# Memory's output projection of twelve token tiles by seven products per pair of tiles, its weights partly loaded again for each pair

## The chip, the cores and the metric

The kernel runs on one core of one Trainium2 chip. The metric is the time of one execution on the device in microseconds, the median of several runs. The program is one launch; all stages follow each other on the same five engines: TensorE (PE), VectorE (DVE), ScalarE (ACT), GpSimd (POOL) and SyncE (SP, which here only issues DMAs).

## The reference, cut to what matters

One layer of an encoder: a mixing block, cross attention to 256 memory tokens, and a SwiGLU feed-forward network, each with a residual. There are 2048 tokens of width 1024, four memory heads of width 128, and a feed-forward width of 2816. The change is in the last line of the middle part, the product with `w_mem_out` (512 x 1024).

```python
h = h + jnp.einsum('bsc,cd->bsd', jnp.concatenate([fox, pool], axis=-1), w_out[l])

hn = rmsnorm(h, g_mem_q[l])
...
pm = jax.nn.softmax(sc, axis=-1).astype(mv.dtype)
mo = jnp.einsum('bhsm,bmhd->bshd', pm, mv).reshape(B, S, MEM_WIDTH)
h = h + jnp.einsum('bsc,cd->bsd', mo, w_mem_out[l])

hn = rmsnorm(h, g_ffn[l])
gu = jnp.einsum('bsd,df->bsf', hn, w_gate_up[l])
```

## The kernel before, in words

**The product.** Every large product is done in words of `fp32r`: an operand is split into a rounded high word (a cast on ACT) and the rest as a low word (`sub_hi`, a subtraction on DVE), and `mm3` (lines 57 to 62) multiplies high by high (L60), high by low (L61) and low by high (L62). So one step of a product is three matmuls of 128 x 128 by up to 512 columns.

**The stages.** First come the projections and the forgetting attention (FoX) with the pooling. Then comes the memory stage, in which the change lies. Then the feed-forward network (FFN), whose products are themselves done by Strassen's seven products over halves of tokens and features; its first products are the `bk` matmuls.

**The memory stage** is one loop over the 16 token tiles of 128 tokens (n = 0 to 16 before). It is a software pipeline that is written out by hand: PE and SP run in program order (`with in_order(EN.SP)`), and the order on DVE, ACT and POOL is left to a scheduler. In iteration n stand, for different tiles: `query_norm(n)` (24 matmuls, the query projection), `ffn_turn(n-5)` (8 transposes of the finished tile, whose results go to DRAM as `hTd` for the FFN), `load_tile(n+1)` and `out_fox(n+1)` (the residual `h1` is loaded from DRAM into one of six buffers, and the output projection of FoX is added to it), `mem_values` for a pair of tiles (its result, `mo`, is split on the way out of PSUM), `softmax(n-1)`, `weights_tm(n-2)` (8 transposes of the softmax's weights `pm`), `mem_out(n-4, 0)` and `mem_out(n-4, 1)` (the projection that the change is about), `query(n+1)` (sum of squares on ACT, 8 transposes) and `query_t(n)` (4 transposes).

`mem_out(i, a)` gives the 512 columns a of tile i: four heads by `mm3`, 12 matmuls into a bank of the tag `mm` (two of them), and one DVE add of the bank to `h1`. With a = 1 the tile is finished: it is stored (`h2d`) and normed for the FFN (`hn`). The eight pieces of `w_mem_out` lie split in SBUF (`wm`).

**The tail.** In the last iterations the token operands of the FFN are prepared beside the memory stage: `token_ops` loads four raw pieces of 128 x 512 for each of four groups j from `hTd` (`xraw`, two buffers of 1 MB), and splits them and their sums and differences on ACT and DVE into the slabs `qs`, `kh`, `kl`, `cb`; two of the results (s3, s4) go to DRAM by POOL. Which call of `tokens(1)` stands where in the loop sets when SP reaches these loads. `weights_raw` loads the first FFN weight (`graw`, 1 MB) and `weight_ops` prepares it. After the last `mem_out` the FFN's `bk` matmuls begin.

## Time and profile before

| what | us |
|---|---|
| median of 3 runs (2565.06 to 2567.35) | 2566.49 |
| the profiled execution | 2566.67 |
| its span in the profile | 2565.0 |
| PE busy in the span | 2532.6 |
| DVE busy | 1702.0 |
| ACT busy | 1248.6 |
| POOL busy | 802.2 |

The granted TensorE clock was 0.999 of full speed over the span. "Busy" counts an instruction from its start to its modelled end; matmuls overlap, so the distance from start to start is what one of them takes. "Idle before" in brackets is the time that an engine waited ahead of an instruction, with what ended the wait. The DMA share is the mean busy share of the core's 16 DMA engines.

### The profile page before, as it was taken

The page shows a single profiled execution, that of the slowest core. Times are in us where ns is not written, and L with a number is a line of the kernel's source. Part 1 is how long each engine was busy: PE and PEld are TensorE (multiplying, and loading weights), DVE is VectorE, ACT ScalarE, POOL GpSimd, SP SyncE. Part 2 cuts the span into 40 slices and gives each one's busy share as a digit, 9 for nine tenths or more (in the row PEclk, how much of TensorE's full clock was granted, in tenths as well). Part 3 has the DMA queues.
Part 4 walks back from the last instruction along what each step waited for, and adds up shares of the span by engine and source line. Part 5 has one row for each costly group of instructions (what it writes and reads, how often), then busy time and mean ns, then how long its engine had stood idle before and what let it go on. Part 6 is the DMA issues. An engine that isn't in the chain of part 4 may idle for free.

```text
span 2565.0 us, 36894 instructions
## 1 busy us (share of the span) xinstructions
PE 2532.6 (99%) x13133; PEld 2176.9 (85%) x13133; DVE 1702.0 (66%) x2943; ACT 1248.6 (49%) x2375; POOL 802.2 (31%) x1075
## 2 busy tenths in 40 slices
PE   8999999999999999999999999999999999999999
PEld 7999999978888878888778888888888888888887
DVE  6444376569999975555777777756766666665554
ACT  6454452158888865444543433334543333333443
POOL 3334240035455433333334545430001222222000
PEclk9999999999999999999999999999999999999999
DMA  6443375346445242222465455447773332334766
GB/s 244 128 122 117 110 227 175 128 135 166 124 113 160 61 133 80 86 78 87 177 223 183 170 180 189 152 162 268 248 263 119 112 115 103 120 106 169 237 207 205
DMA packets 204777, 396.20 MB, mean 154 GB/s; under 512 B 24368, under 2 KB 99888, under 8 KB 193840
## 3 DMA queue, kind: packets, MB, share of 16 engines
q1 hardware_dynamic: 175088, 296.30, 35.9%
q0 software_dynamic: 29504, 97.54, 9.9%
q8 instruction: 103, 1.69, 0.3%
q14 instruction: 82, 0.67, 0.1%
HBM read 268.85 MB, written 124.91 MB: 154 GB/s over the span
## 4 chain that ended last, share of the span: by engine, by line
PE 84%; issue 9%; DVE 3%; DMA 2%; ACT 1%; POOL 1%; SPq 0%; POOLq 0%; DVEq 0%; ACTq 0%
PE bk L60 13%; PE bk L62 13%; PE bk L61 13%; PE acc L752 5%; PE sps L689 5%; PE tp L767 4%; PE zps L60 4%; PE zps L61 4%; PE zps L62 4%; PE mmps L62 3%; PE mmps L60 3%; PE mmps L61 3%; PE oo L62 1%; PE oo L60 1%; PE oo L61 1%
## 5 line engine op out<-in xcount | busy, mean ns | idle before, releaser
L55 DVE TENSOR_TENSOR ww<-draw,ww 128x512 fp32r<-128x512 f32 x308 | 204.7, 703 | 156.1 <-ACT ww L178 155.7
L178 ACT CAST ww<-draw 128x512 fp32r<-128x512 f32 x308 | 179.4, 620 | 219.6 <-PE bk L62 176.4
L55 DVE TENSOR_TENSOR ww<-graw,ww 128x512 fp32r<-128x512 f32 x220 | 175.9, 806 | 105.9 <-ACT ww L178 105.5
L61 PE MATMUL bk<-ww,ww 128*128 128x512 f32 x616 | 239.6, 389 | 0.0
L60 PE MATMUL bk<-ww,ww 128*128 128x512 f32 x616 | 239.6, 389 | 0.0
L62 PE MATMUL bk<-ww,ww 128*128 128x512 f32 x616 | 239.6, 389 | 0.0
L178 ACT CAST ww<-graw 128x512 fp32r<-128x512 f32 x220 | 135.9, 622 | 180.4 <-PE bk L62 159.4
L55 DVE TENSOR_TENSOR pl<-tp,ph 128x512 fp32r<-128x512 f32 (+3 forms) x298 | 177.8, 599 | 24.1 <-ACT ph L783 22.4
L702 ACT ACTIVATE s<-s,mx 128x1024 f32<-128x1024 f32 (+2 forms) x192 | 173.8, 906 | 4.2 <-DVE mx L696 2.3
L60 PE MATMUL zps<-wh,xhi 128*128 128x386 f32 x512 | 175.7, 343 | 0.1
L61 PE MATMUL zps<-wl,xhi 128*128 128x386 f32 x512 | 173.6, 339 | 0.0
L62 PE MATMUL zps<-wh,xl 128*128 128x386 f32 x512 | 173.2, 338 | 0.0
L767 PE MATMUL tp<-ident,s 128*128 128x128 f32 x1088 | 171.5, 273 | 1.7 <-DVE pl L55 1.1
L783 ACT CAST ph<-tp 128x512 fp32r<-128x512 f32 (+3 forms) x298 | 149.8, 515 | 33.4 <-PE tp L767 28.6
L767 PEld LDWEIGHTS tp<-ident,s 128*128 128x128 f32 x1088 | 133.0, 140 | 31.2 <-DVE pl L55 6.4
L62 PE MATMUL bk<-qs,ww 128*128 128x512 f32 x352 | 137.2, 390 | 1.1 <-DVE ww L55 1.1
L60 PE MATMUL bk<-qs,ww 128*128 128x512 f32 x352 | 137.9, 392 | 0.3 <-ACT s L1318 0.3
L1399 POOL DMA_DIRECT2D out_dram<-o x32 | 17.3, 542 | 382.6 <-DVE o L1396 376.8
L61 PE MATMUL bk<-kh,ww 128*128 128x512 f32 x352 | 137.0, 389 | 0.0
L60 PE MATMUL bk<-kl,ww 128*128 128x512 f32 x352 | 136.9, 389 | 0.0
L61 PE MATMUL bk<-cb,ww 128*128 128x512 f32 x352 | 136.9, 389 | 0.0
L62 PE MATMUL bk<-kl,ww 128*128 128x512 f32 x352 | 136.9, 389 | 0.0
(548 smaller groups left out, 7234.7 us busy)
## 6 DMA issues: line engine op xcount, KB each, us to landing
graw<-in_w_gu_dram SPq DMA_DIRECT2D x44, 1024.0 KB, 5.5
draw<-in_w_down_dram SPq DMA_DIRECT2D x66, 256.0 KB, 4.1
xl<-in_xT_dram SPq DMA_DIRECT2D x64, 256.0 KB, 4.6
qkT<-st SPq DMA_DIRECT2D x64, 256.0 KB, 2.7
wdr<-in_w_down_dram SPq DMA_DIRECT2D x22, 512.0 KB, 4.3
vd<-cb SPq DMA_DIRECT2D x16, 512.0 KB, 3.2
xr<-in_x_dram SPq DMA_DIRECT2D x16, 512.0 KB, 3.3
qs<-qkT SPq DMA_DIRECT2D x8, 1024.0 KB, 6.8
```

The costliest lines, as they stand in the source:

```text
L55: (eng or dve).tensor_tensor(out=lo, in0=src, in1=f(hi), op=ALU.subtract)
L60: pe.matmul(ps, lhsT=sh, rhs=mh, start=first, stop=False, skip_group_check=goes_on)
L61: pe.matmul(ps, lhsT=sh, rhs=ml, start=False, stop=False, skip_group_check=goes_on)
L62: pe.matmul(ps, lhsT=sl, rhs=mh, start=False, stop=last, skip_group_check=goes_on)
L178: act.copy(hi, raw)
L689: pe.matmul(ps[:, :wn], lhsT=qs[:, i * P:(i + 1) * P], rhs=kk[:, 512 * c:512 * c + wn], start=(a == 0), stop=(a == 1))
L702: act.activation(s[:, sl], s[:, sl], AF.Exp, bias=ng, scale=-1.0, accum_out=l[:, q, g:g + 1])
L752: pe.matmul(acc[:, qa * P:], lhsT=v[:, j, :], rhs=pm[:, qa * P:], start=state["n"] == 1, stop=state["n"] == 2 * nk)
L767: pe.transpose(tp[:, q * P:(q + 1) * P], unit["rows"][q][:, j * P:(j + 1) * P], ident[:])
L783: act.copy(ph[:, sl], tp[:, sl])
L1399: pool.dma_start(out[rows_, cs], o)
```

## The change

Tiles 0 to 11 are taken in six pairs r. For a pair, the product of (two tiles of tokens x two halves of the heads) with (two halves of the heads x two halves of the columns) is done by seven products in place of eight; each is 2 steps of `mm3`, 6 matmuls. A pair has 42 matmuls where it had 48. Tiles 12 to 15 stay as they were (`mem_plain`).

- `mem_out(r, n)` runs one of four `STEPS`: two products each, the last step one. A product accumulates into one of two banks, `mb0` and `mb1`, which live through the pair; after each product DVE adds the bank, as it then stands, to one quarter of the output. The pair's steps stand in the half iterations of two iterations: steps 0 and 2 where `mem_out(n-4, 1)` was, steps 1 and 3 early in the next iteration.
- The token operands of a step (x11, x12, s1 to s4, x22) are made and split by `mem_ops` from the raw output of `mem_values`, one step ahead.
- The weight operands are made once in n = 0 to 3 (`mem_out_weights`): b11, t2 and t3 stay in SBUF (`HELD`), b21, t1, b22, t4 and b12 are stored in DRAM (`wmd`). `load_sent` loads one of the `SENT` operands, 1 MB, ahead of each step, into the single buffer `wms`. For the last pair and the plain tiles they go to other places as well (the `h1` buffers, and those of t2 and t3).
- The `h1` buffers become three. A tile's `h1` after FoX is stored to DRAM again (`h1d`), and `residual` loads it (`res`, two buffers) when its pair is summed. `put_stores` issues these stores and those of `h2d` and `hTd` from SP; before, POOL issued the latter two. In the tail some are left to POOL.
- In the loop `weights_tm` now stands before `softmax`, `ffn_turn` takes tile n-6, `load_tile` runs two tiles ahead, and the loop ends at n = 15. The calls of `tokens(1)` and of the loads in the tail stand in another order.

The core of the diff:

```diff
-        def mem_out(i, h1, mo, a):
-            ...
-            for k in range(MH):
-                mm3(ps[:], (mo[0][:, k, ts], mo[1][:, k, ts]), (wm[k, a][0][:], wm[k, a][1][:]),
-                    k == 0, k == MH - 1)
-            dve.tensor_tensor(out=h1[:, as_], in0=ps[:], in1=h1[:, as_], op=ALU.add)
+        HELD, SENT = ("b11", "t2", "t3"), ("b21", "t1", "b22", "t4")
+        STEPS = ((("x11", "b11", 0, True, (0, 0)), ("x12", "b21", 1, True, (0, 0))),
+                 (("s2", "t2", 0, False, (0, 1)), ("s1", "t1", 1, True, (1, 1))),
+                 (("s3", "t3", 0, False, (1, 1)), ("s4", "b22", 1, False, (0, 1))),
+                 (("x22", "t4", 0, False, (1, 0)),))
+        def sent_place():
+            return w4.tile([P, 2, 2, 512], F32R, tag="wms", name="wms", bufs=1)
+        def mem_out(r, n):
+            p_ = pairs[r]
+            for x_, w_, bk, begins, (t, a) in STEPS[n]:
+                if begins:
+                    p_[bk] = bigp.tile([P, 512], F32, tag=f"mb{bk}", name=f"mb{bk}", bufs=1)
+                ps = p_[bk]
+                for c in range(2):
+                    mm3(ps[:], (p_[x_][0][:, c], p_[x_][1][:, c]), wm_part(w_, c), begins and c == 0, c == 1, not begins)
+                o = p_["o"][t][:, a * 512:(a + 1) * 512]
+                dve.tensor_tensor(out=o, in0=ps[:], in1=o, op=ALU.add)
+            if n < 3:
+                mem_ops(r, n + 1)
+            if r < R_ - 1 or n == 0:
+                load_sent(SENT[(n + 1) % 4])
+            elif n == 1:
+                load_sent("b22")
+                load_sent("t4", place2([h1p.tile([P, 2, 512], F32R, tag="h1", name="wms", bufs=3) for _ in range(2)]))
+                load_sent("b21", held_place("t2"))
+            elif n == 2:
+                load_sent("b12")
+                load_sent("b22", held_place("t3"))
...
-            h1 = h1p.tile([P, D], F32, tag="h1", name="h1", bufs=6)
+            h1 = h1p.tile([P, D], F32, tag="h1", name="h1", bufs=3)
...
+            R = NT // 2 - 1
+            mem_out(R - 2, 3)
             tokens(1)
-            weights_tm(pmd.pop(NT - 1), *pts[NT // 2 - 1], 1)
-            out_mem(NT - 3, 1)
+            mod[R - 1] = mem_values(*pts.pop(R - 1), True)
+            for t in (13, 14, 15):
+                ends[t] = residual(t // 2, t % 2, "h1" if t < 15 else "xop")
+            put_stores()
+            tokens(1)
+            head_raw = weights_raw(0, wdp, "wd")
```

The queue of SP, where the order matters most, in the steady part. Before, an iteration has two loads (`h` is the residual tile, `v` a piece of FoX's output):

```order
L1009 DMA h_13666<-h1d_137 128x1024
L642 DMA v<-catT_125 128x4x128
L1009 DMA h_13853<-h1d_138 128x1024
L642 DMA v<-catT_126 128x4x128
L1009 DMA h_14074<-h1d_139 128x1024
```

Now the same tiles' iterations have the weight loads (`wms`, 128 x 2048 words), the residuals and the stores between them:

```order
L1009 DMA h_14481<-h1d_141 128x1024
L642 DMA v<-catT_126 128x4x128
L1220 DMA res<-h1d_135 128x1024
L1172 DMA wms<-wmt1d 128x2048
L1220 DMA res<-h1d_136 128x1024
L1172 DMA wms<-wmb22d 128x2048
L1286 DMA h1d_140<-h_14250 128x1024
L1286 DMA hTd_11738<-hst 128x4x128 x2
L1009 DMA h_14687<-h1d_142 128x1024
L1172 DMA wms<-wmt4d 128x2048
L1172 DMA wms<-wmb21d 128x2048
L1286 DMA h1d_141<-h_14481 128x1024
```

Each iteration has two weight loads, and each of them is issued when PE has done with the operand that lies in `wms`.

In the tail, SP's queue before had the token loads (`xraw`; two rows of x2 are one group j), and `graw` after the first two groups:

```order
L1009 DMA h_14669<-h1d_142 128x1024
L912 DMA xraw<-hTd_11737 128x512 x2
L912 DMA xraw<-hTd_11738 128x512 x2
L912 DMA xraw<-hTd_11737 128x512 x2
L912 DMA xraw<-hTd_11738 128x512 x2
L960 DMA graw<-in_w_gu_dram 128x2048
L912 DMA xraw<-hTd_11737 128x512 x2
L912 DMA xraw<-hTd_11738 128x512 x2
L912 DMA xraw<-hTd_11737 128x512 x2
L912 DMA xraw<-hTd_11738 128x512 x2
```

Now, from the first group's second half on:

```order
L912 DMA xraw<-hTd_11738 128x512 x2
L1172 DMA wms<-wmb22d 128x2048
L1176 DMA wms<-wmt4d 128x512 x4
L1176 DMA wms<-wmb21d 128x512 x4
L1286 DMA h1d_142<-h_14687 128x1024
L1286 DMA hTd_11739<-hst 128x4x128 x2
L1220 DMA res<-h1d_139 128x1024
L912 DMA xraw<-hTd_11737 128x512 x2
L912 DMA xraw<-hTd_11738 128x512 x2
L1172 DMA wms<-wmb12d 128x2048
L1176 DMA wms<-wmb22d 128x512 x4
L912 DMA xraw<-hTd_11737 128x512 x2
```

and to its end:

```order
L912 DMA xraw<-hTd_11738 128x512 x2
L1220 DMA res<-h1d_140 128x1024
L1220 DMA res<-h1d_141 128x1024
L1220 DMA res<-h1d_142 128x1024
L1286 DMA h2d_153<-res 128x1024
L960 DMA graw<-in_w_gu_dram 128x2048
L912 DMA xraw<-hTd_11737 128x512 x2
L912 DMA xraw<-hTd_11738 128x512 x2
```

Three of the four token groups and `graw` moved behind the weight loads, and the last group behind `graw`.

On DVE, the last operations of the memory stage before. The four `h<-mmps` rows are the adds of tiles 14 and 15; `graw`, `t` and `ww` are the FFN's first weight:

```order
L973 TENSOR_TENSOR graw<-graw 128x4x128
L55 TENSOR_TENSOR ww_15205<-mops,ww_15204 128x512
L55 TENSOR_TENSOR ww_15261<-graw,ww_15261 128x512
L55 TENSOR_TENSOR ww_15205<-mops,ww_15204 128x512
L973 TENSOR_TENSOR t_15252<-graw,t_15250 128x512
L55 TENSOR_TENSOR ww_15257<-t_15250,ww_15257 128x512
L973 TENSOR_TENSOR graw<-graw,t_15252 128x4x128
L55 TENSOR_TENSOR ww_15254<-t_15252,ww_15254 128x512
L1106 TENSOR_TENSOR h_14482<-mmps,h_14482 128x512 x2
L1106 TENSOR_TENSOR h_14669<-mmps,h_14669 128x512 x2
```

Now the operations on the last token group (`xraw`, `cb`, `kh`) stand there; the `res<-mmps` rows are the adds of tiles 14 and 15:

```order
L913 TENSOR_TENSOR xraw<-xraw 128x512
L973 TENSOR_TENSOR t_15484<-graw,t_15482 128x512
L913 TENSOR_TENSOR xraw<-xraw 128x512
L55 TENSOR_TENSOR cb<-xraw,kl 128x512
L913 TENSOR_TENSOR xraw<-xraw 128x512
L55 TENSOR_TENSOR ww_15486<-t_15484,ww_15486 128x512
L913 TENSOR_TENSOR xraw<-xraw 128x512
L55 TENSOR_TENSOR kh<-xraw,qs 128x512
L55 TENSOR_TENSOR ww_15489<-t_15482,ww_15489 128x512
L973 TENSOR_TENSOR graw<-graw 128x4x128
L973 TENSOR_TENSOR graw<-graw,t_15484 128x4x128
L1237 TENSOR_TENSOR res<-mmps,res 128x512
```

The eleven rows ahead of the first add belong to the last group and to the first weight; before, the group's operations were all ahead of these rows.

## The prediction

> **What bounds the kernel now.** I read the page first. Its busy line says that TensorE has almost no idle time in the whole span.

> ```profile
> span 2565.0 us, 36894 instructions
> PE 2532.6 (99%) x13133; PEld 2176.9 (85%) x13133; DVE 1702.0 (66%) x2943; ACT 1248.6 (49%) x2375; POOL 802.2 (31%) x1075
> ```

> A mean over stages doesn't price a change in one of them, so next came the windows of the memory stage: its start (n=0 to 3), its steady part, its tail and the first feed-forward products. The columns are the busy time of PE, PEld, DVE, ACT and POOL with instruction counts, then granted clock, DMA share and GB/s.

> ```profile
> 955.00:980.00 25.00, 25.00 (x134) 21.13 (x133) 11.56 (x18) 8.54 (x20) 7.19 (x9) 1.00 0.28 95
> 980.00:1005.00 25.00, 24.78 (x136) 20.80 (x136) 18.24 (x30) 17.39 (x41) 9.87 (x12) 1.00 0.32 106
> 1050.00:1075.00 25.00, 25.00 (x143) 21.77 (x142) 12.98 (x22) 10.29 (x22) 9.15 (x13) 1.00 0.23 85
> 1100.00:1125.00 25.00, 25.00 (x145) 21.84 (x145) 13.44 (x20) 11.06 (x25) 8.34 (x11) 1.00 0.20 74
> 1255.00:1260.00 5.00, 4.08 (x20) 3.47 (x21) 4.60 (x9) 3.39 (x11) 3.77 (x5) 1.00 0.96 315
> 1285.00:1290.00 5.00, 4.67 (x21) 3.44 (x20) 4.63 (x9) 2.24 (x4) 0.05 (x1) 1.00 0.98 325
> 1290.00:1295.00 5.00, 5.00 (x24) 4.14 (x23) 1.90 (x3) 0.00 (x0) 0.55 (x1) 1.00 1.03 397
> 1300.00:1305.00 5.00, 4.74 (x21) 3.59 (x21) 5.00 (x9) 4.97 (x9) 0.69 (x1) 1.00 1.04 368
> ```

> In the steady part PE has no gap, DVE is half idle and the DMA engines carry 74 to 85 GB/s: there a matmul less is time less. The tail is another stage: the DMA engines are full in stretches (share near 1 at 315 to 397 GB/s), and DVE is nearly so.

> A busy PE is not PE at its peak, so a matmul's price is the distance of starts in the timeline. These rows of PE are the last of one `mem_out` half; the columns are start, duration, instruction.

> ```profile
> 1062.85 0.39 PE L60 MATMUL mmps<-wm11h,ww 128*128 128x512 f32 x1
> ...
> 1064.66 0.39 PE L62 MATMUL mmps<-wm31h,ww 128*128 128x512 f32 x1
> 1064.89 0.60 PE L878 MATMUL tp<-ident,mq 128*128 128x128 f32 x4
> 1065.24 0.47 PE L60 MATMUL mmps<-qs,hT 128*128 128x512 f32 x1
> ```

> From 1062.85 to 1064.89 are nine matmuls: 0.227 us each, though each lasts 0.39. Four transposes take 0.35; I take 0.87 for eight (two times 0.35, and the dearer first matmul behind).

> Last, the PE timeline of the tail, with what ended each idle time in brackets.

> ```profile
> 1245.29 0.63 PE L878 MATMUL tp<-ident,mq 128*128 128x128 f32 x4 [1.15 <-POOL hr L71]
> 1245.68 0.47 PE L60 MATMUL mmps<-qs,hT 128*128 128x512 f32 x1
> ...
> 1255.92 0.66 PE L878 MATMUL tp<-ident,pm 128*128 128x128 f32 x4 [1.75 <-DVE hst L942]
> ...
> 1280.90 1.25 PE L941 MATMUL tp<-ident,hn 128*128 128x128 f32 x8 [0.80 <-DVE pTl L55]
> ...
> 1296.42 0.39 PE L60 MATMUL bk<-qs,ww 128*128 128x512 f32 x1
> ```

> I put t = 0 at the row of 1245.68, the start of `query_norm(15)`. The first feed-forward matmul (`bk`) comes 50.7 us later, and PE idles only 2.6 us between in these rows. So the tail is PE-bound too now, but barely.

> **The products.** Six pairs of tiles give up 8 products of 2 x 3 matmuls for 7, so 36 matmuls go: 36 x 0.227 = 8.2 us. Up to t = 0 it is more: before had done tiles 0 to 10 there (264 matmuls), after has done five pairs and the first step of the sixth (222). 42 x 0.227 = 9.5 us; one `ffn_turn` of eight transposes goes behind t = 0 as well, 0.9; and the 1.15 us at 1245.29 is the wait for the Square of the last tile, which I take as gone since the operations of DVE and ACT around it are re-dealt (zero if not). Sum up to t = 0: -11.5 us, or -10.4. [...] This trace has 227 ns in a stage without gaps, so the measurement stands.

> **The weights on the way.** Each pair loads four 1 MB operands through the one buffer `wms`. A load is issued behind the PE's last use of the operand before, and must have landed when the next product begins. SP is in order, so a load that waits holds all behind it: `res`, the `h` tile, the stores. Nothing in the before kernel loads so; the nearest rows are DMA issues of the page and of the steady part (the last number is the median us to landing).

> ```profile
> graw<-in_w_gu_dram SPq DMA_DIRECT2D x44, 1024.0 KB, 5.5
> h2d<-h POOLq DMA_DIRECT2D x9, 512.0 KB, 3.0
> h<-h1d SPq DMA_DIRECT2D x9, 512.0 KB, 3.7
> ```

> The cover is the PE work between: at the shortest place (t1, behind the first step of a pair) 4 transposes (0.35), `query_norm` (24 x 0.227 = 5.45), 8 transposes (0.87) and the product on the held t2 (6 x 0.227 = 1.4), 8.1 us; elsewhere 9 to 10. Against 5.5 us for a load of that size it holds; my value is zero, the bounds zero and, at a landing of 9.0, six times 0.9 = 5 us. A pair is two iterations, and the same transposes of `ffn_turn` show its length:

> ```profile
> 1047.01 1.03 PE L941 MATMUL tp<-ident,hn 128*128 128x128 f32 x8
> ...
> 1091.70 1.03 PE L941 MATMUL tp<-ident,hn 128*128 128x128 f32 x8
> ```

> 44.7 us for two, so 22.35 for one, in which 80 GB/s are 1.8 MB. It rises by two weights of 1.05 MB, `res` and the `h1d` store to near 4.9 MB, or 220 GB/s, under the full rates above.

> The prices of what DVE and ACT get, from the groups of the steady part and the page (mean ns behind the comma):

> ```profile
> L1106 DVE TENSOR_TENSOR h<-mmps,h 128x512 f32<-128x512 f32 x17 | 11.8, 692 | 10.0 <-PE mmps L62 9.5
> L178 ACT CAST ww<-graw 128x512 fp32r<-128x512 f32 x220 | 135.9, 622 | 180.4 <-PE bk L62 159.4
> ```

> DVE gets, per pair, three adds of 512 columns more and nine operations of 256. At no more than 0.69 each, 8 us per 45 us, where it is half idle: nothing. In n=0 to 3 the eight operands cost 8 more casts (ACT, 5 us) and 16 more DVE operations (11 us), beside the idle half shown by the windows 955 to 1005: I take +0.5, bounds 0 and 3.

> **The tail.** Here is my main term. Before, the token loads were early on SP:

> ```profile
> 1225.22 8.89 SPq L912 DMA_DIRECT2D xraw<-hTd  x8
> 1251.42 0.33 SPq L960 DMA_DIRECT2D graw<-in_w_gu_dram  x1
> 1252.59 8.03 SPq L912 DMA_DIRECT2D xraw<-hTd  x8
> ```

> All four `xraw` groups (1 MB each) were issued by t = 15. After, by the order of SP, only j=0 goes ahead of b22; b22 waits for PE to finish the second step of pair 5, at t = 9.2 (`query_norm` 5.45, transposes 0.87, 12 matmuls 2.72). Behind it in one queue stand b22, t4, b21, the `h1d` and `hTd` stores, `res` of tile 12 (held until t = 19.6, when PE has freed its slot), `xraw` j=1, b12, b22 again, `xraw` j=2, three `res`, an `h2d` store, `graw` and, last, `xraw` j=3. By tile sizes that is 13.1 MB, and POOL's s3, s4, `h2d` and `hTd` stores add 3.1: 16.2 MB. The full-share windows above have 315 to 397 GB/s; their mean is 351, and I take 0.36 MB/us because this queue is mostly large loads. From 10.3 (issue and first data a microsecond behind 9.2) 45 us: j=3 lands at t = 55.

> What hangs on it is DVE's order. The timeline of DVE gives its pace, and how its last operations lie now:

> ```profile
> 1275.96 0.68 DVE L1106 TENSOR_TENSOR h<-mmps,h 128x512 f32<-128x512 f32 x1
> 1276.56 0.68 DVE L913 TENSOR_TENSOR xraw<-xraw 128x512 f32<-128x512 f32 x1
> 1277.16 0.68 DVE L55 TENSOR_TENSOR cb<-xraw,kl 128x512 fp32r<-128x512 f32 x1
> ...
> 1289.84 0.68 DVE L1106 TENSOR_TENSOR h<-mmps,h 128x512 f32<-128x512 f32 x1
> 1291.18 0.69 DVE L1106 TENSOR_TENSOR h<-mmps,h 128x512 f32<-128x512 f32 x1 [0.66 <-PE mmps L62]
> ```

> One operation per 0.60 us. Now DVE is through with the tokens before the last four adds, and from 1291.18 it waits for PE. After, the first add of tile 14 (`res<-mmps`) stands behind eleven operations on j=3 and the head's weights: 55.3 + 11 x 0.60 = 62. PE has two `mm` banks, so tile 15 waits for that add; then its 24 matmuls, 5.45. The first `bk` comes at t = 67.7 instead of 50.7: +17.0. At 0.40 MB/us j=3 lands at 51 and `bk` comes at 63.5 (+13); at 0.33 at 72 (+21).

> *A rule on this gap:* PE would stand idle for some 10 us ahead of tile 15. The longest idle time quoted here is 1.75 us and the granted clock stays at 1.00 behind it, so no row of before prices a long one; I take nothing. [...]

> **Sum.** The profiled execution took 2566.7 us (span 2565.0 and 1.7 around it), 0.2 above the median of three. 2566.7 - 11.5 + 0.5 + 17.0 = 2572.7 us.

> **Rivals.**

> *The tail is hidden (faster).* If j=3 lands before t = 38, then 11 operations and tile 15's matmuls still end by 50.7, and the change keeps its 11 us: 2566.7 - 11.5 + 0.5 = 2555.7. For it: PE waited for no `xraw` before. Against: 16.2 MB by t = 38 need 0.58 MB/us, and no window shows over 0.40. It needs the program to spread these loads otherwise than in one queue. Chance 0.15.

> *DVE sets the tail, not the loads (about the same).* If the DMA engines drain faster than their rows, `bk` waits for DVE alone: the 2.6 us of PE's waits in the quoted rows grow by about 15 more operations of 0.60 behind t = 0 (three adds, the splits of pair 5, and the operations on j=0, which had begun before), 9 us less what they cover, and `bk` comes at t = 57 to 62: +6 to +11, net -5 to 0, 2562 to 2567. For it: 397 GB/s in one window. Against: the windows with small pieces have 315 and 325. Chance 0.25. [...] The trace's best stretch is 397.

> *The weight loads come late in every pair (much slower).* If a 1 MB load beside `res`, `h` and the stores takes over 8.1 us from issue, PE waits up to four times per pair and what is saved goes back. At 9 us it is the 5 us above, on t1 alone; at 10 us t1 loses 1.9 and the other three about 0.5 each, 3.4 a pair, 20 us in all. On the forecast that makes 2578 to 2593. For it: one buffer and one queue for all of them. Against: 5.5 us measured for a load of this size. Chance 0.2.

> **How the numbers follow.** The forecast (loads set the tail, steady loads hidden) has 0.4, with its own range from 0.40 and 0.33 MB/us: 2568 to 2577, or to 2580 with the start's 3 us. About 0.2% (5 us) is what a measurement of this kernel can tell from no change. Faster: the hidden tail's 0.15 and the best third of the DVE case, 0.08: 0.23. Same (2561.4 to 2571.6): the rest of that case, 0.17, and 0.16 of the forecast: 0.33. Slower: 0.24 of the forecast and 0.2 for late loads: 0.44. The range leaves out most of the hidden tail below and half of the late loads above: 2559 to 2582. The point is the sum, 2572.7.

> **What would show it.** In the profile after: `mmps`/`mb` starts still 0.227 us apart; no PE wait for `wms` in the steady pairs (one is the late-load rival, and its length its price); DMA at some 200 GB/s there; `query_norm(15)` 11 us earlier than 1245.7; then the DMA engines near full from there on, `xraw` j=3 as the last load, and PE idle ahead of tile 15 behind DVE's `res<-mmps`. I am wrong if `bk` starts before t = 57, or if `query_norm(15)` isn't at least 8 us earlier.

## The result, and the profile after

The change makes the kernel slower: 2585.91 us (median of six runs, 2583.83 to 2591.71) against 2566.94 us for the kernel before (six runs on the same chip), a ratio of 1.0079 with a 95% interval of 1.0068 to 1.009. The forecast was 2572.7 us and its range ended at 2582: the sign was right, the size was not.

The page of the changed kernel, to be set against the busy line and span of before:

```profile
span 2590.0 us, 37138 instructions
PE 2538.2 (98%) x13097; PEld 2176.5 (84%) x13097; DVE 1739.4 (67%) x3031; ACT 1267.1 (49%) x2425; POOL 784.7 (30%) x1054
PEclk9999999999999999999989999999999999999999
```

There are 36 matmuls less and PE's busy time is nevertheless 5.6 us longer. The digit 8 in the clock's row, in the slice from 1295 to 1360 us, shows one reason: part of the matmuls ran at a lower clock (0.50 from 1305.15 to 1311.98 and from 1332.46 to 1339.28).

The same windows as before, in the same order (busy PE, PEld, DVE, ACT, POOL; clock, DMA share, GB/s):

```profile
955.00:980.00 25.00, 23.69 (x122) 19.52 (x121) 15.87 (x26) 10.83 (x24) 9.31 (x12) 1.00 0.80 277
980.00:1005.00 25.00, 22.99 (x125) 19.53 (x124) 18.04 (x28) 14.13 (x37) 11.16 (x14) 0.93 0.77 274
1050.00:1075.00 25.00, 25.00 (x147) 21.85 (x146) 15.96 (x28) 12.38 (x28) 5.54 (x7) 1.00 0.69 242
1100.00:1125.00 25.00, 25.00 (x132) 21.21 (x131) 16.87 (x29) 10.65 (x24) 6.12 (x8) 1.00 0.85 280
1255.00:1260.00 5.00, 4.27 (x18) 4.14 (x19) 5.00 (x9) 1.83 (x3) 3.15 (x4) 0.50 0.87 292
1285.00:1290.00 5.00, 2.98 (x16) 2.16 (x15) 4.97 (x9) 2.86 (x5) 1.54 (x3) 1.00 1.03 422
1290.00:1295.00 5.00, 4.08 (x31) 3.64 (x31) 2.56 (x5) 2.01 (x4) 1.90 (x3) 1.00 1.03 405
1300.00:1305.00 5.00, 0.50 (x3) 0.07 (x1) 5.00 (x9) 1.84 (x3) 1.10 (x2) 1.00 0.13 53
```

The steady part (1050 to 1125) still has no gap on PE, at 242 to 280 GB/s. Each of the other places has lost some: the start (955 to 1005) has gaps of 1.3 and 2.0 us, and the tail has a stretch at half clock (1255), one in which the DMA engines are full (1285 to 1295), and one in which PE does almost nothing while DVE is busy throughout (1300).

PE's timeline, from the start of `query_norm(15)` to the feed-forward products:

```profile
1241.49 0.48 PE L60 MATMUL mmps<-qs,hT 128*128 128x512 f32 x1
...
1252.91 0.63 PE L878 MATMUL tp<-ident,pm 128*128 128x128 f32 x4 [2.06 <-DVE hst L942]
...
1255.73 1.08 PE L878 MATMUL tp<-ident,pm 128*128 128x128 f32 x4 [2.19 <-ACT kl L178]
...
1306.97 0.80 PE L60 MATMUL mmps<-wmb,ww 128*128 128x512 f32 x1 [6.47 <-DVE res L1237]
1307.56 0.63 PE L61 MATMUL mmps<-wmb,ww 128*128 128x512 f32 x1
1307.99 0.63 PE L62 MATMUL mmps<-wmb,ww 128*128 128x512 f32 x1
...
1314.90 0.39 PE L60 MATMUL bk<-qs,ww 128*128 128x512 f32 x1
...
1333.31 0.79 PE L62 MATMUL bk<-qs,ww 128*128 128x512 f32 x1 [1.39 <-DVE ww L55]
```

`query_norm(15)` starts 4.2 us earlier than before, not 11; `bk` comes 73.4 us behind it, not 50.7; and the span ends 1275.1 us behind `bk` (2590.0 less 1314.9) where it was 1268.6. The wait forecast ahead of tile 15 is there, 6.47 us for DVE's add. Behind it the matmuls at first start 0.43 us apart, half the pace of the 0.227 of before, and tile 15's 24 take 7.93 us in place of 5.45.

This profile is that of the slowest of the six runs. Two more profiles of the unedited kernel (below) show which parts of it repeat. The span cut at three points, in us: the start is n = 0 to 3 (`query_norm(0)` to `query_norm(4)`), the pairs are n = 4 to 14, the tail is from `query_norm(15)` to the first `bk`.

| kernel | `query_norm(0)` at | start | pairs | tail | behind `bk` | span |
|---|---|---|---|---|---|---|
| before | 947.0 | 56.1 | 242.6 | 50.7 | 1268.6 | 2565.0 |
| after | 946.6 | 61.2 | 233.7 | 73.4 | 1275.1 | 2590.0 |
| after, second profile | 945.4 | 59.3 | 233.4 | 74.0 | 1272.8 | 2584.9 |
| after, third profile | 946.5 | 60.4 | 233.3 | 73.8 | 1274.4 | 2588.4 |
| no weight loads | 946.3 | 62.1 | 232.7 | 62.5 | 1274.5 | 2578.1 |
| no loads, hardly any making | 947.1 | 59.8 | 232.6 | 62.1 | 1274.8 | 2576.5 |
| the same, softmax first | 946.1 | 56.5 | 232.7 | 61.7 | 1274.1 | 2571.0 |
| adds first | 945.9 | 59.6 | 233.4 | 63.3 | 1277.9 | 2580.1 |
| buffers of 13 and 14 swapped | 946.0 | 62.0 | 233.3 | 72.4 | 1269.3 | 2583.0 |
| filled wait | 947.1 | 60.5 | 233.6 | 70.5 | 1273.7 | 2585.4 |
| five pairs | 946.5 | 61.6 | 234.3 | 57.5 | 1269.6 | 2569.6 |
| five pairs, last version | 946.5 | 57.6 | 234.6 | 56.7 | 1268.8 | 2564.2 |

Over the three profiles of the changed kernel the pairs win 8.9 to 9.3 us; the start loses 3.2 to 5.1, the tail 22.7 to 23.3, and what lies behind `bk` 4.2 to 6.5. The second, near the median, adds up as -1.5 (earlier `query_norm(0)`) + 3.2 - 9.2 + 23.3 + 4.2 = +20.0 against a measured +19.9.

**The tail's loads.** SP's timeline (start, duration with its waits, instruction):

```profile
1250.88 0.32 SPq L1172 DMA_DIRECT2D wms<-wmb22d  x1
...
1264.88 2.86 SPq L912 DMA_DIRECT2D xraw<-hTd  x4
...
1271.05 4.78 SPq L912 DMA_DIRECT2D xraw<-hTd  x4
...
1287.95 1.88 SPq L912 DMA_DIRECT2D xraw<-hTd  x4
1290.87 21.77 SPq L1439 DMA_DIRECT2D xr<-s3d  x4
...
1318.67 1.58 SPq L960 DMA_DIRECT2D graw<-in_w_gu_dram  x2
```

The order is the one read from the program: b22 at t = 9.4, then `xraw` j=1, j=2 and, last, j=3 at t = 46.5. Two more readings, the waits of SP in this stretch and the window from b22's issue to j=3's landing:

```profile
SPq L1439 <- DMA h2d<-res: 20.1, 1, 20.1
SPq L912 <- DMA s4d<-xraw: 7.5, 1, 7.5
```

```profile
1251.50:1299.50 48.00, 38.89 (x203) 31.04 (x204) 38.14 (x60) 24.61 (x52) 16.75 (x22) 0.93 0.98 367
```

The 7.5 us are spent ahead of j=3: its buffer holds j=1 until the store of that group's s4 has landed. In these 48 us the engines are 98% full at 367 GB/s, 17.6 MB. The last piece of j=3 is issued at 1289.35 and lands 10.1 us later, at 1299.4. DVE's timeline shows what follows (the bracket names a store that landed just before that piece):

```profile
1299.60 0.69 DVE L913 TENSOR_TENSOR xraw<-xraw 128x512 f32<-128x512 f32 x1 [1.29 <-DMA hTd<-hst]
...
1306.23 0.68 DVE L1237 TENSOR_TENSOR res<-mmps,res 128x512 f32<-128x512 f32 x1
```

DVE resumes on j=3 at t = 58.1, does eleven operations, and begins the add of tile 14 at t = 64.7.

**Behind `bk`.** The row of 1290.87 is the new one. SP stands 20.1 us at the load of `xr`, because its buffer lies over the residual of tile 14, which has to be stored as `h2d` first; before, `xr` went out at 1277.43. Behind it in the queue stands the second feed-forward weight (`graw`, 1318.67; before, 1299.57). Its casts come late, PE waits 1.72 us for ACT and 1.39 for DVE at 1331 to 1333 (before had 1.08 for DVE there and none for these casts of ACT), and half clock follows (0.50 from 1332.46 to 1339.28).

**The start.** PE's first two longer waits there are at 960.25 (1.25 us, for POOL's `mq`) and in n=2, where before had none:

```profile
991.07 1.05 PE L878 MATMUL tp<-ident,mq 128*128 128x128 f32 x4 [2.01 <-DVE hT L55]
```

What ACT and DVE did in that wait:

```profile
988.11 0.48 ACT L1077 ACTIVATE pm<-scps,ng 128x256 f32<-128x256 f32 x1
...
988.56 1.07 ACT L1036 ACTIVATE junk<-h 128x1024 f32<-128x1024 f32 x1
...
989.60 1.08 ACT L880 CAST hT<-tp 128x512 fp32r<-128x512 f32 x2
```

```profile
987.84 1.02 DVE L55 TENSOR_TENSOR wmt<-wmr,wmt 128x512 fp32r<-128x512 f32 x1
988.78 0.68 DVE L1102 TENSOR_TENSOR wmr<-wmr,wmr 128x512 f32<-128x512 f32 x1
...
990.23 1.29 DVE L55 TENSOR_TENSOR hT<-tp,hT 128x512 fp32r<-128x512 f32 x2
```

PE needs `hT`. On ACT its cast stands behind the exponentials of softmax (`pm`), which are later than before since `weights_tm` was put ahead of softmax; on DVE its subtraction stands behind the making of the weight operands. So two queues hold it; the runs below take them apart.

**The pairs.** The page's rows for the slowest and the fastest of the weight loads (the last number is the median us from issue to landing):

```profile
wms<-wmt1d SPq DMA_DIRECT2D x6, 1024.0 KB, 6.8
wms<-wmt4d SPq DMA_DIRECT2D x5, 1024.0 KB, 4.7
```

They land under the 8.1 us of cover, and PE waits for none of them between 1040 and 1235. The rival of late loads is false there; only in the full tail does PE wait for two (1.50 us for b12, 0.37 for b22).

### The profile page after: what moved, and what is told of

The parts are those of the page before. It is cut to its first block, busy times and chain, and to the rows that moved or that the text cites. A ratio compares the mean times of both kernels' runs of the same rounds, so it can differ in the third digit from the quotient of the medians.

```text
span 2590.0 us, 37138 instructions
## 1 busy us (share of the span) xinstructions
PE 2538.2 (98%) x13097; PEld 2176.5 (84%) x13097; DVE 1739.4 (67%) x3031; ACT 1267.1 (49%) x2425; POOL 784.7 (30%) x1054
## 4 chain that ended last, share of the span: by engine, by line
PE 69%; issue 8%; DMA 3%; DVE 3%; ACT 1%; POOL 1%; SPq 0%; POOLq 0%; DVEq 0%; ACTq 0%
PE bk L62 13%; PE bk L61 13%; PE bk L60 13%; PE acc L752 5%; PE sps L689 5%; PE tp L767 4%; PE mmps L60 2%; PE mmps L62 2%; PE mmps L61 2%; PE oo L62 1%; PE oo L60 1%; PE oo L61 1%; PE tp L878 1%; PE zp L61 1%; PE zp L60 1%
## 5 line engine op out<-in xcount | busy, mean ns | idle before, releaser
L55 DVE TENSOR_TENSOR ww<-draw,ww 128x512 fp32r<-128x512 f32 x308 | 205.6, 705 | 155.6 <-ACT ww L178 155.4
L178 ACT CAST ww<-draw 128x512 fp32r<-128x512 f32 x308 | 179.2, 620 | 218.6 <-PE bk L62 170.7
L55 DVE TENSOR_TENSOR ww<-graw,ww 128x512 fp32r<-128x512 f32 x220 | 177.4, 812 | 109.1 <-ACT ww L178 108.8
L62 PE MATMUL bk<-ww,ww 128*128 128x512 f32 x616 | 239.6, 389 | 0.0
L60 PE MATMUL bk<-ww,ww 128*128 128x512 f32 x616 | 239.6, 389 | 0.0
L178 ACT CAST ww<-graw 128x512 fp32r<-128x512 f32 x220 | 135.9, 621 | 189.9 <-PE bk L62 162.9
L55 DVE TENSOR_TENSOR pl<-tp,ph 128x512 fp32r<-128x512 f32 (+3 forms) x298 | 177.6, 598 | 24.1 <-ACT ph L783 22.4
L60 PE MATMUL zps<-wh,xhi 128*128 128x386 f32 x512 | 175.7, 343 | 0.1
L62 PE MATMUL zps<-wh,xl 128*128 128x386 f32 x512 | 173.2, 338 | 0.0
L60 PE MATMUL bk<-qs,ww 128*128 128x512 f32 x352 | 138.7, 394 | 2.2 <-ACT ww L178 1.7
L62 PE MATMUL bk<-qs,ww 128*128 128x512 f32 x352 | 138.2, 393 | 1.4 <-DVE ww L55 1.4
L60 PE MATMUL bk<-kl,ww 128*128 128x512 f32 x352 | 136.9, 389 | 0.0
L62 PE MATMUL bk<-kl,ww 128*128 128x512 f32 x352 | 136.9, 389 | 0.0
L61 PEld LDWEIGHTS bk<-ww,ww 128*128 128x128 f32 x616 | 115.6, 188 | 24.6 <-DVE ww L55 0.6
## 6 DMA issues: line engine op xcount, KB each, us to landing
graw<-in_w_gu_dram SPq DMA_DIRECT2D x44, 1024.0 KB, 5.4
wdr<-in_w_down_dram SPq DMA_DIRECT2D x22, 512.0 KB, 4.4
vd<-cb SPq DMA_DIRECT2D x16, 512.0 KB, 3.3
xr<-in_x_dram SPq DMA_DIRECT2D x16, 512.0 KB, 3.4
qs<-qkT SPq DMA_DIRECT2D x8, 1024.0 KB, 6.8
```

The source lines that it names most:

```text
L55: (eng or dve).tensor_tensor(out=lo, in0=src, in1=f(hi), op=ALU.subtract)
L60: pe.matmul(ps, lhsT=sh, rhs=mh, start=first, stop=False, skip_group_check=goes_on)
L61: pe.matmul(ps, lhsT=sh, rhs=ml, start=False, stop=False, skip_group_check=goes_on)
L62: pe.matmul(ps, lhsT=sl, rhs=mh, start=False, stop=last, skip_group_check=goes_on)
L178: act.copy(hi, raw)
```

## The experiments

The theory after the result: the loss has four parts that are in series, the start (queue places), the bytes of the tail, the clock behind its waits, and a load held by a buffer. The rivals: that the weight loads alone cost it, or the making of the operands alone.

**No weight loads.** An operand that would be loaded is replaced by one that is held; no load is left.

```diff
-            t_ = place or sent_place()
-            ...
-            wm_now[op] = t_
+            held = wm[HELD[len(op) % 2 + 1]]
+            wm_now[op] = [held[:, c, e_] for c in range(2) for e_ in range(2)]
```

> The changed kernel without any load of a weight operand: every product on a sent operand is done with one of the held ones (so its output isn't the reference's). The operands are still made and stored in n=0 to 3. It takes 24 loads of 1 MB away, five of them in the tail. Theory A (a chain of buffers sets the tail: group 1 of the tokens is issued late on SP, behind a residual that waits for PE; group 3 needs its buffer, and the add of tile 14 stands behind group 3): group 1's issue stays near t = 23 and only landings get shorter, 5 to 8 us less, 2578 to 2581. Theory B (the bytes set the tail, as predicted): 5.2 MB at 0.4 MB/us less ahead of group 3, 13 us less, about 2573. By the late-load rival also every pair gets shorter; the trace of the changed kernel has no PE wait for a load in the pairs, so I expect the pair's 43.7 us to stay within 0.4.

Measured: 2579.05 us (2574.96 to 2579.91), ratio 1.0046 [1.0033, 1.0059]. The window, the first `bk` and the longest waits of PE in the tail of this kernel:

```profile
1251.50:1299.50 48.00, 38.23 (x209) 31.92 (x210) 41.70 (x65) 23.88 (x51) 16.30 (x23) 0.96 0.67 245
```

```profile
1303.55 0.39 PE L60 MATMUL bk<-qs,ww 128*128 128x512 f32 x1
```

```profile
PE tp L878 <- DVE hst L942: 5.2, 2, 3.0
PE mops L60 <- ACT kl L178: 2.8, 1, 2.8
```

The tail falls from 73.4 to 62.5 us: 11 of its 23 lost us go with the loads. The other 12 remain at 245 GB/s: PE's waits there add up to some 10 us (2.9 before), a stretch at half pace comes with them (matmuls 0.43 us apart from 1283.45 to 1286.01), and 2.3 are work that the change moved behind t = 0 (6 matmuls and 8 transposes); 62 is the upper end that the prediction gave the rival "DVE sets the tail". The last piece of j=3 lands at t = 38.7 here (issued at 1275.30, 4.4 us to landing), 19 us earlier than with the loads, and `bk` comes only 11 us earlier: another chain takes over. The time is in the range of theory A, not at B's 2573. The pairs gain 0.6 to 1.0 us, so loads that PE never waits for still cost 0.1 to 0.2 us each pair. Start and the part behind `bk` do not change: neither is a matter of the loads.

**Hardly any making either.** The sums and the stores of the operands in n = 0 to 3 go as well, and five of the eight splits; the held ones are split from raw weights (this changes the output too).

```diff
-            put("b11", b11)
-            put("b21", b21)
+            split(wm["b11"][:, c, 0], wm["b11"][:, c, 1], b11)
             yield
-            ...
+            split(wm["t2"][:, c, 0], wm["t2"][:, c, 1], b21)
```

> As e1_no_reload, and the weight operands are not made either: three raw pieces per half are cast and split, no sums, no stores to DRAM (output isn't the reference's). Theory A: the 7 us that n=0 to 4 lost (PE waiting for mq and hT behind the operations and stores of the operands, and the half clock behind one wait) come back, so 6 to 8 us under e1. Theory B: the making is hidden by idle time, within 2 us of e1.

Measured: 2578.18 us (2576.69 to 2579.71), 1.0046 [1.0033, 1.0059]: nothing beside the one above. In n=0 the wait for POOL is gone (12.56 us, as before the change); in n=2 PE still waits as long, with three of the eight splits left of the making:

```profile
990.14 0.80 PE L878 MATMUL tp<-ident,mq 128*128 128x128 f32 x4 [2.02 <-DVE hT L55]
```

So the amount of the making alone is not the cause in n=2.

**Softmax first in n = 0 to 3.** The order of before, in the changed kernel:

```diff
+                i = n - 1
+                if n < 4 and 0 <= i < NT:
+                    pmd[i] = softmax(*qtd.pop(i))
                 i = n - 2
...
-                if 0 <= i < NT:
+                if 4 <= n and i < NT:
```

> The changed kernel with softmax ahead of the softmax weights' transposes again in n=0 to 3, as before the change; all else as in the changed kernel, the making of the weight operands too. Theory A (what n=2 and n=3 lost is this swap: ACT's exponentials and the Square stand ahead of the casts of hT, PE waits for hT, and the clock drops behind the wait): n=2 and n=3 go from 17.2 and 16.0 us to about 15, 3 to 4 us less, 2582 to 2583. Theory B (the operations of the operands in front of hT on DVE are the cause): n=2 stays above 16.5, within 1 us of 2586. The run without making, where n=2 still took 17.15, speaks for A.

Measured: 2589.44 us (2584.45 to 2590.57), 1.0084 [1.0071, 1.0098], no less than unedited; the start is 59.8 us, inside the 59.3 to 61.2 of the unedited profiles. n=2 keeps its loss (16.90 us); PE now waits 1.91 us for `pTl`, on DVE behind the making and two reductions. n=3 took 14.57, but the second and third profile of the unedited kernel have 14.76 there too, so that says nothing. (Two later runs with this order and the making, three edits together and five pairs, have 58.3 and 61.6 us: one profile tells a start to no better than 1.5 us or so.) The order alone is not the cause either.

**Both.** No loads, hardly any making, and softmax first: the two edits above together.

> e2_no_making (no weight operand made, none loaded; output not the reference's) with the softmax order of e5_start_order. Each of the two alone left n=2 at 17 us. If they are two queues on one path, each hiding behind the other, both away give n=2 about 14.9 and n=3 about 14.9, as before the change, and 3 to 4 us less than e2: 2574 to 2575. If something third holds n=2 (the h1 stores, three buffers for h1), it stays above 16.5.

Measured: 2576.29 us (2573.24 to 2577.05), 1.0036 [1.0023, 1.0049]. The start is 56.5 us against 56.1 before the change, n=2 is 15.54 (16.5 to 18.0 in every profile with the changed order), and `query_norm(15)` comes at 1235.17, 10.5 us earlier than before. Each cause hid behind the other: taken away singly, neither shows in n=2. The gain of the products that the prediction had up to this point is nearly there once the start is clean. The profile is that of the fastest of the five runs; the median is 1.9 us below that of the run before, where 3 to 4 were expected, and the two intervals overlap, so it is the rows of n=2 that carry this, not the medians.

**Earlier `xraw`.** The load of j=1 is issued with that of j=0, so that the later groups move up.

```diff
+                for k in (0, 1) if j == 0 else () if j == 1 else (j,):
+                    raws[k] = raw_in_v(k)
+                    load_raw(0, k, raws[k])
+                yield from token_ops(0, j, raws[j], SLABS, load=False)
```

> The changed kernel with the load of token group 1 issued right behind that of group 0, ahead of the weight loads of the last pair; nothing else moves on SP. Theory A (buffer chain): group 1's operations and its s4 store end earlier, group 3 is no longer held for its buffer and is issued right behind graw, 6 to 7 us earlier; bk 4 to 7 us earlier, 2579 to 2582. Theory B (bytes): the same bytes, group 3 still last, lands within 2 us of before; 2584 to 2587.

Measured: 2587.19 us (2584.47 to 2589.35), 1.008 [1.0067, 1.0093]. j=3 goes out at 1282.73, 5 us earlier and without the wait for its buffer, and yet its last piece lands at 1300.6 (issued at 1285.20, 15.4 us to landing), no earlier than the 1299.4 of the changed kernel; the tail is 73.1 us as it was. So it is the bytes and not the buffer that set this landing, as in theory B. The wait ahead of tile 15 is only 1.22 us here, but PE waits 4.05 us for DVE's `xop` and 3.14 for `ww` ahead of it. The earlier issue of one load did not help here: its last piece landed 1.2 us later, in a stretch in which the changed kernel's engines are 98% full.

**Adds first.** The operations on j=3 and the head's weights come behind the adds of tiles 14 and 15.

```diff
             for i in range(NT - 2, NT):
                 for a in range(2):
                     mem_plain(i, a)
+            head = weight_ops(head_raw)
             put_stores(pool)
+            tokens(3)
```

> The changed kernel with its loads where they are, but the operations on token group 3 and on the head's weights written behind the last four products, so that the order of DVE has the adds of tiles 14 and 15 ahead of those on group 3. Theory A (the wait is one of DVE's order): PE does tile 15 while group 3 lands, the 6.5 us wait and the half clock behind it shrink, the FFN's xr loads, which wait for tile 14's store, are issued some 7 us earlier, and the stall at the second FFN weight goes: 8 to 14 us less, 2572 to 2578. Theory B (group 3's landing sets the start of bk whatever the order): bk waits for the same landing, at most 3 us less, 2583 to 2586.

Measured: 2582.78 us (2581.77 to 2588.05), 1.0071 [1.0058, 1.0085]. The tail is 63.3 us, 10 less, but the time only 3, just below theory B's range and not in A's. PE then waits:

```profile
1302.24 0.39 PE L60 MATMUL bk<-qs,ww 128*128 128x512 f32 x1
...
1315.22 0.80 PE L60 MATMUL bk<-qs,ww 128*128 128x512 f32 x1 [7.38 <-ACT s L1526]
```

ACT's timeline shows why: its copy `s` of the first product stands behind casts of `xr`.

```profile
1311.78 1.20 ACT L178 CAST x22h<-xr 128x512 fp32r<-128x512 f32 x2 [1.80 <-DMA xr<-hTd]
...
1314.59 0.58 ACT L1526 COPY s<-bk 128x512 f32<-128x512 f32 x1
```

And SP's, why the casts are late: `xr` again waits for its buffer.

```profile
1287.12 19.83 SPq L1448 DMA_DIRECT2D xr<-s3d  x4
```

Most of the gain went to the next wait in the row.

**Buffers of tiles 13 and 14 swapped,** so that `xr` lies over the residual of tile 13, which is stored earlier:

```diff
-            for t in (13, 14, 15):
+            for t in (14, 13, 15):
```

> The changed kernel with the residuals of tiles 13 and 14 in each other's buffer. The FFN's second xr load lies over the buffer of tile 14 and waited 20 us on SP for its store, all loads of the first FFN steps behind it. Theory A (this queue makes the 6 us that are lost behind the first bk): the xr loads and graw are issued 5 to 14 us earlier, the stall at the second FFN weight goes, 4 to 6 us less, 2580 to 2582. Theory B (they are late because the DMA engines are full until bk begins): at most 2 us less, 2584 to 2586.

Measured: 2584.71 us (2580.51 to 2587.37), 1.0067 [1.0053, 1.0081]. SP's wait is shorter:

```profile
1291.02 13.17 SPq L1439 DMA_DIRECT2D xr<-s3d  x4
```

Of these 13 us, 6.4 are the wait for `h2d` (20.1 unedited). Behind `bk` the span has 1269.3 us, against 1272.8 to 1275.1 in the three unedited profiles and 1268.6 before: the held load is the cause of that part. The run with the earlier `xraw` agrees: there the same wait is 6.8 us, and behind `bk` the span has 1269.5. The medians differ by 1.2 us only, inside the spread of both and in the range of theory B; in this profile the start took 62.0 us and the wait ahead of tile 15 was 7.52.

**The wait filled.** 26 matmuls whose result nobody reads stand ahead of tile 15, so that PE isn't idle there.

```diff
+                if i == NT - 1:
+                    warm = bigp.tile([P, MH, MEM], F32, tag="sc", name="warm", bufs=1)
+                    ...
+                    for _ in range(26):
+                        pe.matmul(wv, lhsT=..., rhs=..., start=True, stop=True)
```

> The changed kernel with 26 more matmuls of 512 columns on PE, into a bank that nothing reads, between the products of tile 14 and tile 15, where PE waits 6.5 us and then works at half clock. Theory A (the clock falls because PE stands still, and that is a price of its own beside the wait): the 24 matmuls of tile 15 start 0.227 us apart from the first on, they take 5.5 us in place of 7.9, and bk begins 2 us earlier by as much, though PE has 5.9 us of work more; 2583 to 2585. Theory B (the slow stretch is due to something else, the full DMA engines or SBUF): tile 15's matmuls stay 0.43 apart, and the time is the same or up to 1 us more.

Measured: 2587.06 us (2586.93 to 2590.1), 1.0082 [1.0068, 1.0096]. PE's timeline:

```profile
1299.00 6.05 PE L1420 MATMUL warm<-wmb 128*128 128x512 f32 x26
...
1306.09 0.50 PE L60 MATMUL mmps<-wmb,ww 128*128 128x512 f32 x1 [1.04 <-DVE res L1237]
...
1311.67 0.39 PE L60 MATMUL bk<-qs,ww 128*128 128x512 f32 x1
...
1321.90 0.80 PE L60 MATMUL bk<-qs,ww 128*128 128x512 f32 x1 [4.63 <-ACT s L1522]
```

Tile 15 takes 5.58 us (1306.09 to 1311.67) in place of 7.93: what was lost there is the clock, and the idle time is its cause. The tail is 2.9 to 3.5 us shorter, but the median does not show it; a 4.63-us wait for ACT's copy has come behind `bk`, again with half pace behind it (0.43 us apart from 1322.50 to 1324.63).

**Three together:** softmax first in n = 0 to 3, adds first, buffers swapped.

> e4_adds_first, e5_start_order and e6_xr_slot together. If the three places are separate and each costs what theory A says: 2582.8 (e4) less 3.5 (start) less 5 to 7 (PE's 7.4 us wait for ACT, which stands behind the casts of the late xr loads): 2572 to 2574. If the bytes of the tail set it whatever the order: above 2578.

Measured: 2581.79 us (2581.18 to 2585.35), 1.0063 [1.0051, 1.0076], 8 to 10 us above what the parts added up to. PE waits 6.80 us for ACT's copy, as with the adds alone: the adds moved forward took the place of the token work, whose `s3` products `xr` has to wait for.

**Five pairs.** Only tiles 0 to 9 go in pairs, on top of the three edits; no weight is loaded in the tail, and the first two `xraw` groups are loaded in n=14.

```diff
-        R_ = NT // 2 - 2
+        R_ = NT // 2 - 3
...
+                if n == NT - 2:
+                    early_raw(0)
...
+                if n == NT - 2:
+                    early_raw(1)
```

> e8_three with Strassen's products for five pairs only (tiles 10 and 11 plain: 6 matmuls more, 1.4 us; b21 and b12 loaded into the places of t3 and t2 ahead of n=15, so no weight load is left in the tail) and the token groups 0 and 1 loaded in n=14. By theory A and by the bytes alike the tail gets shorter: 5 MB less and 2 MB earlier behind t = 0, bk 55 to 60 us behind query_norm(15) where the changed kernel has 73; 2563 to 2568, about the time before the change. Above 2572 something else than loads and order sets the tail (the token operations on DVE, which before began 13 us ahead of query_norm(15)).

Measured: 2570.16 us (2566.41 to 2574.99, 11 runs), 1.0013 [1.0005, 1.0022], 2 us above the expected range: 16 of the 19 us are back, at the cost of one pair's six matmuls (1.4 us). The tail is 57.5 us. It has 132 matmuls where before had 120, and one more transposing turn: 12 x 0.227 + 0.9 = 3.6 of the 6.8 us that it has more; waits of 1.84 us for DVE's residual and 3.49 for POOL's `pm` (2.9 in all before) make up most of the rest.

**The start of that kernel,** in two steps. First the operand stores by SP in place of POOL, and softmax first in n=4 too:

```diff
-                    pool.dma_start(wmd[op][:, c], f(o))
+                    stores.append((wmd[op][:, c], f(o)))
...
-                if n < 4 and 0 <= i < NT:
+                if n < 5 and 0 <= i < NT:
```

> e9_five_pairs with the stores of the weight operands issued by SP with the other stores of the loop in place of POOL, and the softmax order of before in n=4 too. Theory A (in n=0 PE waits for mq, which POOL multiplies behind two stores of 0.57 us): n=0 goes from 15.1 to below 14, its clock stays up, so n=1 goes to 13.8; n=4 from 16.6 to about 15.5; 3 to 5 us less than e9: 2565 to 2567. If ACT's casts of the operands hold mq alone, n=0 stays near 15, 2569.

Measured: 2569.45 us (2566.67 to 2571.41), 1.0009 [1.0000, 1.0018]. The start is 58.7 us (61.6); 1.6 of the difference are n=1, 13.76 us without the half pace of the profile before (0.43 us apart from 962.56 to 965.12). n=4, though, takes 18.35 us in place of 16.6, and n=0 still waits 1.75 us for POOL's `mq` (2.35): there the stores were not the main cause. With n=0 at 14.94 and this median, the second case of the expectation is the one that came, ACT's casts; no run takes these away alone.

Then the making at the end of an iteration, behind what PE needs:

```diff
-                if ahead:
-                    next(wsteps)
...
                 qtd[n] = query_t(mqd.pop(n))
+                if ahead:
+                    next(wsteps)
+                    next(wsteps)
```

> e12_sp_stores with the making of the operands written at the end of each of n=0 to 3 in place of two places in its middle, so that DVE and ACT have the iteration's own operations first. If the start's loss is the place of these operations in the queues and not their amount: n=0 to 3 near 12.6, 13.8, 14.9, 14.9 and 6 to 8 us less than e9, 2562 to 2564, under the kernel before. If the amount counts: within 2 us of e12.

Measured: 2569.58 us (2568.53 to 2570.45), 1.0012 [1.0003, 1.002]. The start is 57.1 us, 1.0 above that of before, n=2 is 14.58 for the first time: the same operations, in another place of the same queues. The median does not move beside the one above, which is what was expected if the amount counts; the rows speak for the place, and the time does not show it.

**What was left.** n=4 back to the changed order, and `graw` issued earlier in n=15, since POOL's `pm` and with it PE waited 3.43 us behind its casts:

```diff
+                    head_raw = weights_raw(0, wdp, "wd")
                     tokens(1)
...
-                if n < 5 and 0 <= i < NT:
+                if n < 4 and 0 <= i < NT:
```

> e13 with two more changes: the softmax stands first in n=0-3 only (in n=4 the weight operations first again, as in the changed kernel), and the load of the second FFN weight (graw) is issued in n=15, ahead of the second part of the token work. Theory A (what keeps the mended kernel some 3 us above the kernel before is n=4's 1.75 us and the wait of 3.43 us for POOL's pm behind casts of graw): the step of n=4 is back near 16.6 us (18.35 in e13), the 3.4-us wait is gone or under 1 us, median 2564 to 2567. Theory B (the tail is bound by bytes, so a load moved ahead only pushes xraw or xr back by as much): n=4 is back (-1.75), but the wait for the adds in front of the last tile grows by 2 to 3 us, median 2567.5 to 2569.5.

Measured: 2567.57 us (2564.08 to 2570.44, 11 runs), 1.0001 [0.9992, 1.001]. n=4 is 16.59; the wait for `pm` is 2.0 us. Theory A holds for n=4; of the 3.43 us it got 1.4, and no other wait grew by more than 0.6 (1.8 us ahead of tile 10's second half, as it was; a new one of 0.54 for DVE's `hst`). The median is 0.6 above its range, and inside B's, so the median alone does not decide it.

Last, the token work in n=15 was moved behind tile 10's second half:

```diff
                         slab_op(op)
-                    tokens(1)
...
                     mem_plain(2 * R_, 1)
+                    tokens(1)
```

> e14 with the first part of the token work behind the second half of tile 10, so that the adds of the residuals stand ahead of it on DVE. Theory A (the wait of 1.85 us for DVE's residual is a matter of DVE's order): it falls under 0.5 us, median 1 to 2 us below e14's, 2563 to 2566. Theory B (the gain is given to the next wait, as in e4_adds_first, since the token work is late by as much): ACT's or POOL's wait behind it grows by 1 to 2 us, median within 1 us of e14's.

Measured: 2566.28 us (2564.43 to 2569.91, 11 runs), 0.9999 [0.999, 1.0008]. The waits of PE from 1235 on:

```profile
PE tp L878 <- POOL pm L1083: 2.7, 1, 2.7
PE mmps L60 <- DVE res L1241: 1.9, 1, 1.9
```

The wait for the residual's add did not fall, and neither theory was tried: the order of DVE's instructions came out as it was (only the order of SP and PE is written by hand here), with the first `xraw` operations still ahead of the add. So the run is a repeat of the one before it. Against the kernel before, in the table: start +1.5, pairs -8.0, tail +6.0, behind `bk` +0.2. Eleven runs of each of the last two give no difference from the kernel before that can be told, and no version here beats it.

**The changed kernel twice more,** unedited, to see which of its terms vary:

> The changed kernel once more, unedited: its profiled run above was the slowest of six, 5.8 us over the median, so it is open which of the three terms (up to t=0: -4.2; t=0 to bk: +22.7; behind bk: +6.5) holds the 5.8. Theory A (the term behind bk varies, since it depends on whether the second FFN weight just misses a use): in a run near 2586, span behind bk 1269 to 1271 and the first two terms within 1 us of the ones above. Theory B (the clock's phase behind short waits varies): behind bk still 1274 to 1276, and the two earlier terms 4 to 6 us smaller together.

> A second such run, so that the terms of three profiles of one kernel can be set beside each other: theory A has the terms before bk within 1 us over the three profiles and the spread behind bk; theory B the reverse.

Measured: 2586.61 and 2590.12 us; the terms are in the table. Neither theory has it alone. Between the fastest and the slowest of the three, 5.1 us apart in span, 1.2 lie in when `query_norm(0)` starts, 1.9 in the start, 0.3 in the pairs, 2.3 behind `bk`, and the tail goes the other way by 0.6. A good part is the clock, though not where theory B put it: n=3 takes 16.04 us in the first profile, in which it runs at half clock from 991.1 to 994.5, and 14.76 and 14.77 in the other two, in which it does not; behind `bk` the slowest has 6.8 us at half clock and the fastest 3.4. The tail's +23 is the part that repeats.

## Why the prediction was wrong, step by step

*The products: right, short by 2 us.* Starts are 0.227 us apart still, and a pair without loads takes 43.39 us (two iterations of 22.45 and 20.94) in place of 44.69: 1.30 less, against 6 x 0.227 = 1.36. Over n = 4 to 14 the changed kernel gains 8.9 to 9.3 us, 9.9 without loads; the sum had 10.4, or 11.5 with the wait at 1245.29. That upper value was the one taken, and the wait is indeed gone. What is missing lies in n=4: 12 matmuls fewer should give 2.7 us, and it went from 17.46 to 16.60, 0.9, since PE waits there 0.94 us for DVE's `pTl` and 0.29 for ACT's `mo`. The rest, about 1 us, are the slower steps beside the loads.

*The weights on the way: right.* No wait for `wms` in the steady pairs, landings of 4.7 to 6.8 us under a cover of 8.1, 242 to 280 GB/s where 220 was forecast. The price was zero in waits and 0.6 to 1.0 us over the pairs in slower steps.

*The start, +0.5 with bounds of 0 and 3: failed.* It was +3.2 to +5.1. The step argued from idle halves of ACT and DVE in 25-us windows. The runs showed in its place that the position of the work mattered more than its amount: with the making ahead of `hT` on DVE and softmax behind `weights_tm` on ACT, PE waited in n=2 whichever of the two was taken away (2.02 and 1.91 us); with both taken away the start was 56.5, and with all the making kept but placed last, and softmax first, 57.1 (that run has five pairs and its stores on SP as well). With this loss `query_norm(15)` came 4.2 to 7.6 us earlier, below the 8 that the prediction had named as its own sign of being wrong. The move of `weights_tm` ahead of softmax was in the diff, and was not costed at all.

*The tail, +17: right in mechanism, short by 6.* The chain was the one forecast: full engines, j=3 last, eleven operations of DVE, the add of tile 14, PE waiting. The rate was right (367 GB/s, 0.36 taken). The bytes were short: 17.6 MB passed by the landing where 16.2 were counted. A wait of 7.5 us for the buffer of j=3 was not in the chain, but the run with the earlier `xraw` shows that it did not set the landing. DVE was on j=3 at t = 58.1 and the add came at t = 64.7 for 62, +2.7. Then the clock: tile 15 took 7.93 us for 5.45, +2.5. The sum of the two is 5.2 of the 5.7 missing in the first profile. (Two of the sums are a little off as written, and it does not matter beside this: the terms given for b22's t = 9.2 make 9.0, and those for 67.7 make 67.4.) That the loads are only half of the tail was not seen: without them it is still 12 us longer than before, which is the DVE rival at its upper end, and the forecast had the two as alternatives where one stood behind the other. Its condition for a hidden tail, j=3 landed before t = 38, was all but met in the run without loads (38.7), and the tail was not hidden.

*The gap ahead of tile 15, taken as nothing: failed.* No row of before priced a wait of that length. The wait with PE filled and the wait with PE idle, side by side, give 5.58 and 7.93 us for the same 24 matmuls. Idle, it cost 2.3 us by these, and 2.5 against the 5.45 of the sum. PE was at half clock (0.50) from its start at 1306.97 to 1311.98, 5.0 us: the clock's window from 1305.15 to 1308.56 held 1.59 us of its work and did not bring full clock back, the next one was full and did (last section).

*Behind the first `bk`, nothing: failed.* It was +4.2 to +6.5. The list of SP's queue ended at `xraw` j=3, where the chain was thought to end. The next row of the same queue, the load of `xr`, had a new wait, since its buffer now lay over the residual of tile 14; behind it stood the second feed-forward weight. With the buffers swapped this part is 1269.3, within 0.7 of before.

In the second profile, near the median, the steps add up: `query_norm(15)` comes 7.6 us earlier where the sum had 11.0 (3.4 missing, although `query_norm(0)`, which the change does not touch, happened to come 1.5 early), the tail is 6.3 longer than forecast, and `bk` has 4.2 behind it: 13.9 us, which is what the run lies above the forecast.

*The rivals.* The hidden tail and the late loads in every pair did not happen. The range left out half of the late loads' chance above 2582, and nothing in it stood for a loss at the start and behind `bk` at the same time: the start and the tail came out above the upper bounds they had been given (3 and 21 us), and the part behind `bk` had no bound at all.

## What to carry to other kernels

Idle time in a window is no cover for work that is added to an engine: read the queue, and cost where each new instruction stands ahead of one that TensorE waits for, every moved line included. When a chain in a tail is shortened, the gain goes to the next wait in the row unless that is taken away as well (10 us of tail were won by the adds alone, 3 of them reached the time); when a chain is costed, follow each in-order queue past its end, and look up whose buffer the next load lies over. A wait of PE can cost more than itself: behind the 2.01 us at 991.07 the clock was 0.50 for 3.41 us, behind the 2.02 us at 1289.33 it stayed at 1.00.
